# A two-layer decoder trunk on one core: where the partial sums of paired products are kept, and which engine empties the PSUM banks

## The chip, the core and the metric

The kernel runs on one core of one Trainium2 chip. A core has a matrix engine (TensorE, PE in the profile, with its weight loads as PEld), a vector engine (VectorE, DVE), a scalar engine (ScalarE, ACT), a general engine (GpSimd, POOL) and a queue that only issues transfers (SyncE, SP). Matrix products are accumulated in PSUM, which this kernel uses as eight banks of 128 x 512 float32; everything else lives in SBUF. Each engine works through its own instructions in a fixed order and waits for the others at semaphores. The metric is the time of one execution in microseconds (us).

## What is computed

Two layers over 256 positions of width 2048. Each layer normalises the rows, projects them with one wide matrix into queries, keys, values, the two halves of a spatial gating unit and two sets of gates, runs sliding-window attention and the spatial unit, merges both by the gates, and applies an output projection and a SwiGLU feed-forward part of width 5632.

```python
for l in range(DEPTH):
    h = rms_norm(x, mix_norm[l])
    q, k, v, uv, gate_logits = jnp.split(h @ w_in[l], cuts, axis=-1)
    q = apply_rope(rms_norm(q.reshape(B, S, N_Q_HEADS, HEAD_DIM), q_norm[l]), cos, sin)
    k = apply_rope(rms_norm(k.reshape(B, S, N_KV_HEADS, HEAD_DIM), k_norm[l]), cos, sin)
    branch_a = sliding_window_attention(q, k, v, sinks[l]) @ w_attn_branch[l]
    branch_b = chunked_sgu(jax.nn.gelu(uv), w_spatial[l], ...) @ w_sgu_branch[l]
    gates = jax.nn.sigmoid(gate_logits)
    merged = gates[..., :D_MODEL] * branch_a + gates[..., D_MODEL:] * branch_b
    x = x + merged @ w_out[l]
    h2 = rms_norm(x, ffn_norm[l])
    x = x + (jax.nn.silu(h2 @ w_gate[l]) * (h2 @ w_up[l])) @ w_down[l]
```

## The kernel before

**Products in three parts.** The weights are float32. ScalarE rounds a piece of 256 x 512 weights to a high part (`whi`, line 206), VectorE computes the rest (`wlo`, line 207), and the activations are split in the same way (`uh`, `ul`). One product of a 256-row piece with 128 positions is six matmuls: two blocks of 128 rows, each high by high, low by high and high by low (lines 292 to 294). A full *entry* of the work list does this for both halves of the positions (t = 0, 1), so twelve matmuls into two banks.

**The work list.** Every wide matrix is cut into column chunks of 512, and each chunk is a `Plan`: a list of entries, one for each 256 rows. The method `next` of `Stream` runs ahead of the entry in hand: loads by 7 entries, the splits by 4, sums on the weights by 6. Four buffers hold the split weights, so the split of the entry three places ahead starts when TensorE has left the entry before this one.

**Singles and pairs.** The projections of the first part (keys and values, two chunks of queries, gates, `v` and `u` of the spatial unit) and the two branch projections are single plans of X entries. Output projection, gate and up, and down projection are *pairs*: two column chunks `wa` and `wb`, accumulated in banks a[0], a[1] and b[0], b[1] for the two position halves. In a pair, the first 512 rows of the contraction go through the Strassen-Winograd scheme: seven products P1 to P7 of one block in place of eight, with sums of the weights (`k11` to `k22`, line 194) and of the activations (`sh`, `sl`). The other rows are ordinary entries, G into a and U into b. There are 38 pairs in the kernel.

**The head.** P1, P2, P6, P7 and P4 are the head of a pair. They are interleaved with the last four entries t0 to t3 of the plan in front: t0, P1, P2, t1, P6, t2, P7, t3, P4. P5 and P3 come in the body: G, P5, G, P3, then the other G and all U (in pairs marked `by_unit`, G and U come in twos, so that the last G stands third from the end). P1, P6, P7 and P4 accumulate one after the other in a[1], and ScalarE copies the state behind P1, P6 and P7 into SBUF (`snap`, line 318). The final results are a[0] plus the state behind P1; a[1]; b[0] plus the state behind P6 and P5; b[1] plus the state behind P7. P5 goes into b[1], and VectorE adds it to the state of P6 (line 320). Whoever evicts the pair adds the states: `residual` in a second pass over the same rows (line 821), `hidden` by an addition in front of its own work (line 892).

**Banks.** Four banks (`ps_acc`) serve single plans and pairs, taken in turn; two more (`ps_at`) serve attention and, for every other pair, its banks a. The last two hold transpositions.

**Steps by ticks.** Everything that is not a matmul of a plan (rotation of queries, transpositions, softmax, the spatial unit) is registered with `after(n, ...)` and issued n entries later by `tick`. The order of TensorE's instructions is the program's. The order on the other engines is set when the kernel is built, by a planner that estimates when each instruction is ready, so it can differ from the program's.

**Evictions of the first part.** Keys and queries are scaled out of PSUM by VectorE (line 856) into a buffer of the large pool. They are then squared by ScalarE (line 624), scaled by an inverse square root from GpSimd (line 266), rotated, transposed in blocks (line 360), sent through GpSimd's transfers (line 365) and copied into `qT` (line 676), from which the scores are computed (line 692). The masked scores go to SBUF at line 696, and the values are multiplied at line 731. For gelu, VectorE scales half the argument out of PSUM into a temporary (`xh`, line 747), and ScalarE reads PSUM a second time for the square (line 749); both run one or two ticks behind the product. Gates go out of PSUM through a tanh on ScalarE (line 808).

Of the kernel before, what the change touches and what calls it, by code (L numbers as in the profile page):

```python
# [11 lines left out]
ALU = mybir.AluOpType  # L12
# [42 lines left out]
def hybrid_trunk(ctx: ExitStack, tc: tile.TileContext, x, mix_norm, w_in, q_norm, k_norm, sinks,  # L55
# [37 lines left out]
    class Plan:  # L93


        def __init__(self, key, head, body):
            self.key, self.head, self.body = key, head, body
            self.left = len(head) + len(body)
            self.paired = bool(head)
            self.opened, self.acc, self.snaps, self.calls = set(), {}, {}, None  # L100
# [20 lines left out]
    def pair(key, wa, wb, by_unit=False):  # L121

        h1, h2 = 2 * WINO, 2 * WINO + 1
        l11, l12, l21, l22 = (load_of(w, h, t) for w, h, t in ((wa, h1, "k11"), (wb, h1, "k12"), (wa, h2, "k21"),
                                                              (wb, h2, "k22")))
        k11, k12, k21, k22 = l11[0], l12[0], l21[0], l22[0]
        rest = [h for h in range(wa.shape[0] // (2 * P)) if h // 2 != WINO]  # L130
        g, u = [half(wa, h, "G") for h in rest], [half(wb, h, "U") for h in rest]
        head = [dict(tag="P1", loads=[l11, l12], src=k11), dict(tag="P2", loads=[l21, l22], src=k21),
                dict(tag="P6", loads=[], sums=[(k12, k22, "-", k12), (k11, k11, "+", k12)], src=k11),
                dict(tag="P7", loads=[], src=k12), dict(tag="P4", loads=[], sums=[(k21, k21, "-", k11)], src=k21)]
        p5 = dict(tag="P5", loads=[], sums=[(k11, k22, "-", k11)], src=k11)
        p3 = dict(tag="P3", loads=[], src=k22)
        body = [g[0], p5, g[1], p3] + g[2:] + u
        if by_unit:
            body = [g[0], p5, g[1], p3] + u[:2]
            for i in range(2, len(rest), 2):  # L140
                body += g[i:i + 2] + u[i:i + 2]
        return Plan(key, head, body)
# [18 lines left out]
    entries = []  # L161
    for p in plans:
        if p.head:
            t = [entries.pop() for _ in range(4)][::-1]
            h = p.head
            entries += [t[0], h[0], h[1], t[1], h[2], t[2], h[3], t[3], h[4]]
        entries += p.body

    class Stream:
# [19 lines left out]

        def add(self, upto):  # L190
            while self.summed < min(upto, len(entries)):
                for d, x, op, y in entries[self.summed].get("sums", ()):
                    with tc.issue_after(self.last.ins):
                        self.last = nc.vector.tensor_tensor(out=self.raws[d], in0=self.raws[x], in1=self.raws[y],  # L194
                                                            op=ALU.add if op == "+" else ALU.subtract)
                self.summed += 1

        def split(self, upto):
# [97 lines left out]
    def step():  # L296
        e = entries[stream.at]
        p, tag = e["plan"], e["tag"]
        units = units_at[p.key]
        w = stream.next()  # L300
        if tag in "XGU":
            ps = banks(p, "b" if tag == "U" else "a")
            todo = [(ps[t], block(units, e["h"], t)) for t in range(NT)]
        else:
            sh, sl = units[WINO][2:]
            which, t, form = {"P1": ("a", 1, (0, 0)), "P2": ("a", 0, (1, 0)), "P6": ("a", 1, 1), "P7": ("a", 1, 2),
                              "P4": ("a", 1, (1, 1)), "P5": ("b", 1, 0), "P3": ("b", 0, 3)}[tag]
            todo = [(banks(p, which)[t], (sh[:, form], sl[:, form]) if isinstance(form, int)
                     else block(units, 2 * WINO + form[0], form[1]))]
        for ps, u in todo:  # L310
            add_product(p, ps, u, w)
        a, b = p.acc.get("a"), p.acc.get("b")
        if tag in ("P1", "P6", "P7"):
            if tag != "P7":
                p.snaps["s"] = slot([P, 2, CW], name="snap")
            i = {"P1": 0, "P6": 0, "P7": 1}[tag]
            p.snaps[tag] = p.snaps["s"][:, i, :]
            nc.scalar.activation(p.snaps[tag], a[1], AF.Copy)  # L318
        elif tag == "P5":
            nc.vector.tensor_tensor(out=p.snaps["P6"], in0=b[1], in1=p.snaps["P6"], op=ALU.add)  # L320
# [417 lines left out]
    class Spatial:  # L738
# [3 lines left out]
            self.pl, self.nrm = pl, nrm  # L742
            self.vt, self.sguT = [None] * 2, [None] * 2

        def gelu(self, ps, dst, t):
            xh = temp(name="xh")
            nc.vector.tensor_scalar(out=xh, in0=ps[t], scalar1=self.nrm.rh[t], scalar2=None, op0=ALU.mult)
# [5 lines left out]
            nc.vector.scalar_tensor_tensor(out=dst[:, t, :], in0=sq, scalar=1.0, in1=xh,  # L753
                                           op0=ALU.add, op1=ALU.mult)

        def v(self, c, ps):
            self.vt[c] = vt = slot([P, NT, CW], name="v")
            for t in range(NT):
                after(1 + t, lambda t=t: self.gelu(ps, vt, t))
                after(4 + 3 * t, lambda t=t: self.center(c, t))  # L760

        def center(self, c, t):
# [17 lines left out]
            nc.vector.tensor_tensor(out=vt[:, t, :], in0=vt[:, t, :], in1=self.pl.lnb[:, sl], op=ALU.add)  # L780

        def u(self, c, ps):
            ut = slot([P, NT, CW], name="u")
            for t in range(NT):
                after(1 + t, lambda t=t: self.gelu(ps, ut, t))
# [26 lines left out]
    def residual(key, nxt=None, scale=1.0, store=False):  # L812

        def chunk(j, sums):
            for t in range(NT):
                n = 2 if store and j == NCH - 1 else 1
                w = CW // n
                for i in range(n):
                    sl = slice(j * CW + i * w, j * CW + (i + 1) * w)
                    for part in reversed(sums[t]):  # L820
                        nc.vector.scalar_tensor_tensor(out=xs[:, t, sl], in0=part[:, i * w:(i + 1) * w], scalar=scale,  # L821
                                                       in1=xs[:, t, sl], op0=ALU.mult, op1=ALU.add)
# [15 lines left out]
    for l in range(DEPTH):  # L838
# [4 lines left out]
        for kind, c in FIRST_PART:  # L843
# [7 lines left out]
            if kind in ("v", "u"):  # L851
                (spa.v if kind == "v" else spa.u)(c, ps)
            else:
                dst = slot([P, NT, CW], name=kind)
                for t in range(NT):
                    nc.vector.tensor_scalar(out=dst[:, t, :], in0=ps[t], scalar1=norm.r[t], scalar2=None, op0=ALU.mult)
                att.keys(dst) if kind == "kv" else att.queries(c, dst)
            tick()

# [26 lines left out]
        def hidden(hT, c):  # L886
            hid = slot([P, NT, CW], name="hid")

            def added(sums):
                for x in sums:  # L890
                    if len(x) > 1:
                        nc.vector.tensor_tensor(out=x[1], in0=x[0], in1=x[1], op=ALU.add)  # L892
                return [x[-1] for x in sums]

            def on_gate(sums):
                g = added(sums)
# [5 lines left out]
            def on_up(sums):  # L902
                up = added(sums)
# [57 lines left out]
```

## Time and profile before

| | |
|---|---|
| median of 3 runs (least to most) | 2495.94 us (2494.14 to 2498.18) |
| the profiled execution, its own time | 2499.61 us |
| its span, first to last instruction | 2497.9 us |
| granted TensorE clock, mean | 0.995 |
| weight splits, line 206 and line 207 | 1012 each, mean 1058 and 1219 ns |
| sums on the weights, line 194 | 152, mean 1220 ns |
| ScalarE waiting in line 206 for TensorE | 854.7 us |
| moved by DMA | 501.99 MB, mean 201 GB/s |

The profile is one execution, taken on the core. A row of a group gives line, engine, operation, what is written and read, and durations; matmuls overlap, so the distance from one start to the next says more than the length of one. A row of the timeline gives start, length, engine, line, operation and, in brackets, the idle time in front and who ended it. A row "A <- B" of the waits gives the time A stood idle until B, how often and the longest.

### The profile page before, as it was taken

Reading aid. Unit: us, or ns where it says so; the run is one execution under the profiler, and the core shown is the slowest. Engines: PE = TensorE matmul, PEld = TensorE weight load, DVE = VectorE, ACT = ScalarE, POOL = GpSimd, SP = SyncE. Lnnn points to the kernel's source line nnn. Section 1 sums busy time; section 2 is a strip of 40 time slices with the busy share of each in tenths; the row PEclk is TensorE's granted clock in tenths of the full one; section 3 lists DMA queues with packets and bytes.
Section 4 is the critical chain, followed back from the end, with each engine's and each line's share of the span. In section 5 each row is a group of like instructions: output and inputs, shape, how many; then the busy total and the mean of one; then the engine's idle time right before and its main releaser. Section 6 shows DMA issues by size and latency. Waiting matters only on the chain.

```text
span 2497.9 us, 31092 instructions
## 1 busy us (share of the span) xinstructions
PE 2479.3 (99%) x11142; PEld 2050.1 (82%) x11142; DVE 1905.9 (76%) x2281; ACT 1340.8 (54%) x1658; POOL 379.3 (15%) x735
## 2 busy tenths in 40 slices
PE   9999999999999999999999999999999999999999
PEld 7778888888888888888887888888888888888887
DVE  6686556797987788778866865567878777877787
ACT  5455444565655565555644554445655555655564
POOL 2401212131110111011123012221311101110110
PEclk9999999999999999999999999999999999999999
DMA  8745667667665767576776456775767666665764
GB/s 282 219 140 166 192 202 211 203 211 223 191 221 182 223 192 223 180 218 196 228 217 195 137 168 201 207 207 175 238 193 217 204 199 214 200 221 182 223 186 151
DMA packets 271562, 501.99 MB, mean 201 GB/s; under 512 B 25968, under 2 KB 28624, under 8 KB 271408
## 3 DMA queue, kind: packets, MB, share of 16 engines
q1 hardware_dynamic: 248720, 476.90, 62.2%
q0 software_dynamic: 22368, 22.84, 3.1%
q8 instruction: 87, 1.43, 0.2%
q14 instruction: 67, 0.55, 0.1%
q10 hardware_dynamic: 320, 0.27, 0.0%
HBM read 475.27 MB, written 2.10 MB: 191 GB/s over the span
## 4 chain that ended last, share of the span: by engine, by line
PE 97%; DMA 1%; DVE 1%; issue 0%; ACT 0%; POOL 0%; SPq 0%; DVEq 0%; ACTq 0%
PE acc L292 31%; PE acc L293 31%; PE acc L294 31%; PE po L731 1%; DMA tt<-box 1%; PE psc L692 1%; PE pt L402 1%; PE ppt L721 1%; PE psg L795 0%; POOL tt L365 0%; DVE wlo L207 0%; ACT whi L206 0%; DMA raw<-in_w_in_dram 0%; DVE ul L393 0%; PE pw L591 0%
## 5 line engine op out<-in xcount | busy, mean ns | idle before, releaser
L207 DVE TENSOR_TENSOR wlo<-raw,whi 128x1024 fp32r<-128x1024 f32 (+1 forms) x1012 | 1227.7, 1219 | 518.5 <-ACT whi L206 506.4
L206 ACT ACTIVATE whi<-raw 128x1024 fp32r<-128x1024 f32 (+1 forms) x1012 | 1065.5, 1058 | 1029.5 <-PE acc L294 854.7
L292 PE MATMUL acc<-whi,uh 128*128 128x512 f32 x3204 | 1258.6, 393 | 3.1 <-ACT gate L808 1.8
L293 PE MATMUL acc<-wlo,uh 128*128 128x512 f32 x3204 | 1252.6, 391 | 0.8 <-DVE wlo L207 0.8
L294 PE MATMUL acc<-whi,ul 128*128 128x512 f32 x3204 | 1252.0, 391 | 0.0
L292 PEld LDWEIGHTS acc<-whi,uh 128*128 128x128 f32 x3204 | 604.2, 189 | 128.1 <-ACT gate L808 2.2
L293 PEld LDWEIGHTS acc<-wlo,uh 128*128 128x128 f32 x3204 | 604.2, 189 | 127.6 <-DVE wlo L207 3.8
L294 PEld LDWEIGHTS acc<-whi,ul 128*128 128x128 f32 x3204 | 603.9, 188 | 126.2
L365 POOL DMA_DIRECT2D tt<-box x656 | 321.7, 497 | 1724.1 <-DVE box L360 650.0
L194 DVE TENSOR_TENSOR raw<-raw,raw 128x1024 f32<-128x1024 f32 x152 | 185.4, 1220 | 1.0
L292 PE MATMUL acc<-whi,sh 128*128 128x512 f32 x304 | 118.9, 391 | 0.0
L294 PE MATMUL acc<-whi,sl 128*128 128x512 f32 x304 | 118.4, 390 | 0.0
L293 PE MATMUL acc<-wlo,sh 128*128 128x512 f32 x304 | 118.4, 390 | 0.0
L318 ACT ACTIVATE snap<-acc 128x512 f32<-128x512 f32 x114 | 68.2, 598 | 40.6 <-PE acc L294 40.6
L292 PEld LDWEIGHTS acc<-whi,sh 128*128 128x128 f32 x304 | 57.1, 188 | 11.9
L294 PEld LDWEIGHTS acc<-whi,sl 128*128 128x128 f32 x304 | 57.1, 188 | 11.9
L293 PEld LDWEIGHTS acc<-wlo,sh 128*128 128x128 f32 x304 | 57.1, 188 | 11.5
L821 DVE SCALAR_TENSOR_TENSOR xs<-acc,xs 128x512 f32<-128x512 f32 (+1 forms) x66 | 42.5, 667 | 9.2 <-PE acc L294 8.9
L892 DVE TENSOR_TENSOR snap<-acc,snap 128x512 f32<-128x512 f32 x66 | 45.2, 685 | 4.8 <-PE acc L294 4.8
L821 DVE SCALAR_TENSOR_TENSOR xs<-snap,xs 128x512 f32<-128x512 f32 (+1 forms) x50 | 33.0, 662 | 1.4 <-ACT snap L318 1.3
L905 DVE SCALAR_TENSOR_TENSOR hid<-snap,rr,hid 128x512 f32<-128x512 f32 x44 | 32.5, 739 | 0.0
L709 ACT ACTIVATE pr<-pr,negm 128x128 f32<-128x128 f32 (+1 forms) x64 | 28.2, 442 | 7.9 <-DVE negm L702 7.9
(134 smaller groups left out, 884.7 us busy)
## 6 DMA issues: line engine op xcount, KB each, us to landing
raw<-in_w_in_dram SPq DMA_DIRECT2D x239, 512.0 KB, 4.2
raw<-in_w_up_dram SPq DMA_DIRECT2D x176, 512.0 KB, 5.0
raw<-in_w_gate_dram SPq DMA_DIRECT2D x176, 512.0 KB, 4.4
raw<-in_w_down_dram SPq DMA_DIRECT2D x176, 512.0 KB, 4.5
raw<-in_w_out_dram SPq DMA_DIRECT2D x64, 512.0 KB, 4.7
tt<-box POOLq DMA_DIRECT2D x656, 32.0 KB, 4.3
raw<-in_w_attn_branch_dram SPq DMA_DIRECT2D x32, 512.0 KB, 4.0
raw<-in_w_sgu_branch_dram SPq DMA_DIRECT2D x32, 512.0 KB, 4.5
```

What stands on the lines that cost most here:

```text
L194: self.last = nc.vector.tensor_tensor(out=self.raws[d], in0=self.raws[x], in1=self.raws[y], op=ALU.add if op == "+" else ALU.subtract)
L206: nc.scalar.activation(hi[:, i, :], raw[:, i, :], AF.Copy)
L207: self.last = nc.vector.tensor_tensor(out=lo[:, i, :], in0=raw[:, i, :], in1=hi[:, i, :].bitcast(F32), op=ALU.subtract)
L292: nc.tensor.matmul(ps, a, hi[:, kk, :], start=first and kk == 0, stop=False, skip_group_check=True)
L293: nc.tensor.matmul(ps, a, lo[:, kk, :], start=False, stop=False, skip_group_check=True)
L294: nc.tensor.matmul(ps, b, hi[:, kk, :], start=False, stop=kk == 1, skip_group_check=True)
L318: nc.scalar.activation(p.snaps[tag], a[1], AF.Copy)
L365: nc.gpsimd.dma_start(dst[j * B:(j + 1) * B, i], box[i * B:(i + 1) * B, j])
L709: nc.scalar.activation(pr4[:, h, :nk], pr4[:, h, :nk], AF.Exp, bias=nm_[:, h:h + 1], accum_out=den[:, h:h + 1])
L821: nc.vector.scalar_tensor_tensor(out=xs[:, t, sl], in0=part[:, i * w:(i + 1) * w], scalar=scale, in1=xs[:, t, sl], op0=ALU.mult, op1=ALU.add)
L892: nc.vector.tensor_tensor(out=x[1], in0=x[0], in1=x[1], op=ALU.add)
L905: nc.vector.scalar_tensor_tensor(out=hid[:, t, :], in0=up[t], scalar=norm.rr[t], in1=hid[:, t, :], op0=ALU.mult, op1=ALU.mult)
```

## The change

Which products are computed does not change; where their sums are kept does.

- P5 joins the head and goes into the empty bank a[0]. Five entries of the plan in front are interleaved: t0, P1, t1, P5, t2, P2, P6, t3, P7, t4, P4.
- Behind P5, ScalarE copies P5 from a[0] to SBUF (`kept`) and then a[1] (the state behind P1) into a[0]. P2 accumulates onto that.
- Behind P6 and P7, VectorE reads a[1], adds P5 and writes the two halves of `kept`.
- Behind the second G entry (the first, in pairs by units) ScalarE copies the halves of `kept` into b[0] and b[1], and P3 and the U entries accumulate onto them. All additions at the eviction go.
- The sums on the weights are four differences instead of three and one sum, since the products come in another order.
- Keys, queries and the halves of gelu's argument leave PSUM through ScalarE, the latter at the end of the product; the square is taken from the half in SBUF, and the gelu result overwrites it.

```diff
+        head = [dict(tag="P1", loads=[l11, l12], src=k11),
+                dict(tag="P5", loads=[], sums=[(k11, k12, k11)], src=k11),
+                dict(tag="P2", loads=[l21, l22], src=k21),
+                dict(tag="P6", loads=[], sums=[(k11, k22, k11)], src=k11),
+                dict(tag="P7", loads=[], sums=[(k12, k22, k12)], src=k12),
+                dict(tag="P4", loads=[], sums=[(k21, k21, k11)], src=k21)]
-        body = [g[0], p5, g[1], p3] + g[2:] + u
+        body = g[:2] + [g[2], p3] + g[3:] + u
+        g[1]["then"] = "open"
         if by_unit:
-            body = [g[0], p5, g[1], p3] + u[:2]
+            body = g[:2] + [p3] + u[:2]
+            g[0]["then"] = g[1].pop("then")
...
-            t = [entries.pop() for _ in range(4)][::-1]
+            t = [entries.pop() for _ in range(5)][::-1]
             h = p.head
-            entries += [t[0], h[0], h[1], t[1], h[2], t[2], h[3], t[3], h[4]]
+            entries += [t[0], h[0], t[1], h[1], t[2], h[2], h[3], t[3], h[4], t[4], h[5]]
...
-        if tag in ("P1", "P6", "P7"):
-            if tag != "P7":
-                p.snaps["s"] = slot([P, 2, CW], name="snap")
-            i = {"P1": 0, "P6": 0, "P7": 1}[tag]
-            p.snaps[tag] = p.snaps["s"][:, i, :]
-            nc.scalar.activation(p.snaps[tag], a[1], AF.Copy)
-        elif tag == "P5":
-            nc.vector.tensor_tensor(out=p.snaps["P6"], in0=b[1], in1=p.snaps["P6"], op=ALU.add)
+        if tag == "P5":
+            p.kept = slot([P, 2, CW], name="kept")
+            nc.scalar.activation(p.kept[:, 1, :], a[0], AF.Copy)
+            nc.scalar.activation(a[0], a[1], AF.Copy)
+        elif tag in ("P6", "P7"):
+            nc.vector.tensor_tensor(out=p.kept[:, int(tag == "P7"), :], in0=a[1], in1=p.kept[:, 1, :], op=ALU.add)
+        if "then" in e:
+            for t, ps in enumerate(banks(p, "b")):
+                nc.scalar.activation(ps, p.kept[:, t, :], AF.Copy)
+                p.opened.add(id(ps))
         p.left -= 1
         if e is getattr(p, "last_g", None):
-            p.calls[0]([[a[0], p.snaps["P1"]], [a[1]]])
+            p.calls[0](a)
         if p.left == 0 and p.paired:
-            p.calls[1]([[b[0], p.snaps["P6"]], [b[1], p.snaps["P7"]]])
+            p.calls[1](b)
...
+        def half(self, ps, name):
+            dst = slot([P, NT, CW], name=name)
+            for t in range(NT):
+                nc.scalar.activation(dst[:, t, :], ps[t], AF.Copy, scale=self.nrm.rh[t])
+            return dst
...
-            nc.scalar.activation(sq, ps[t], AF.Square, scale=self.nrm.r[t])
+            nc.scalar.activation(sq, xh, AF.Square, scale=2.0)
...
-                    nc.vector.tensor_scalar(out=dst[:, t, :], in0=ps[t], scalar1=norm.r[t], scalar2=None, op0=ALU.mult)
+                    nc.scalar.activation(dst[:, t, :], ps[t], AF.Copy, scale=norm.r[t])
```

In `residual` the second pass over `snap` goes, and in `hidden` the function `added` with its additions.

More of the change, by code (lines that the diff above doesn't have):

```diff
@@ L99, in __init__ @@
             self.paired = bool(head)
-            self.opened, self.acc, self.snaps, self.calls = set(), {}, {}, None
+            self.opened, self.acc, self.calls = set(), {}, None
             for e in head + body:
@@ L131, in pair @@
         g, u = [half(wa, h, "G") for h in rest], [half(wb, h, "U") for h in rest]
[L132 to L135, printed above, removed]
+        head = [dict(tag="P1", loads=[l11, l12], src=k11),
[4 more added lines that the diff above has]
+                dict(tag="P4", loads=[], sums=[(k21, k21, k11)], src=k21)]
         p3 = dict(tag="P3", loads=[], src=k22)
-        body = [g[0], p5, g[1], p3] + g[2:] + u
+        body = g[:2] + [g[2], p3] + g[3:] + u
+        g[1]["then"] = "open"
         if by_unit:
-            body = [g[0], p5, g[1], p3] + u[:2]
+            body = g[:2] + [p3] + u[:2]
+            g[0]["then"] = g[1].pop("then")
             for i in range(2, len(rest), 2):
@@ L191, in add @@
             while self.summed < min(upto, len(entries)):
-                for d, x, op, y in entries[self.summed].get("sums", ()):
+                for d, x, y in entries[self.summed].get("sums", ()):
                     with tc.issue_after(self.last.ins):
                         self.last = nc.vector.tensor_tensor(out=self.raws[d], in0=self.raws[x], in1=self.raws[y],
-                                                            op=ALU.add if op == "+" else ALU.subtract)
+                                                            op=ALU.subtract)
                 self.summed += 1
@@ L306, in step @@
             which, t, form = {"P1": ("a", 1, (0, 0)), "P2": ("a", 0, (1, 0)), "P6": ("a", 1, 1), "P7": ("a", 1, 2),
-                              "P4": ("a", 1, (1, 1)), "P5": ("b", 1, 0), "P3": ("b", 0, 3)}[tag]
+                              "P4": ("a", 1, (1, 1)), "P5": ("a", 0, 0), "P3": ("b", 0, 3)}[tag]
             todo = [(banks(p, which)[t], (sh[:, form], sl[:, form]) if isinstance(form, int)
@@ L743, in __init__, with gelu @@
             self.vt, self.sguT = [None] * 2, [None] * 2
-        def gelu(self, ps, dst, t):
-            xh = temp(name="xh")
-            nc.vector.tensor_scalar(out=xh, in0=ps[t], scalar1=self.nrm.rh[t], scalar2=None, op0=ALU.mult)
+        def half(self, ps, name):
[3 more added lines that the diff above has]
+            return dst
+        def gelu(self, dst, t):
+            xh = dst[:, t, :]
             sq = temp(name="sq")
-            nc.scalar.activation(sq, ps[t], AF.Square, scale=self.nrm.r[t])
+            nc.scalar.activation(sq, xh, AF.Square, scale=2.0)
             nc.vector.scalar_tensor_tensor(out=sq, in0=sq, scalar=1.0 / GELU_A, in1=xh,
@@ L752, in gelu @@
             nc.scalar.activation(sq, sq, AF.Tanh, scale=2.0 * GELU_C * GELU_A)
-            nc.vector.scalar_tensor_tensor(out=dst[:, t, :], in0=sq, scalar=1.0, in1=xh,
-                                           op0=ALU.add, op1=ALU.mult)
+            nc.vector.scalar_tensor_tensor(out=xh, in0=sq, scalar=1.0, in1=xh, op0=ALU.add, op1=ALU.mult)
         def v(self, c, ps):
-            self.vt[c] = vt = slot([P, NT, CW], name="v")
+            self.vt[c] = vt = self.half(ps, "v")
             for t in range(NT):
-                after(1 + t, lambda t=t: self.gelu(ps, vt, t))
+                after(1 + t, lambda t=t: self.gelu(vt, t))
                 after(4 + 3 * t, lambda t=t: self.center(c, t))
@@ L782, in u @@
         def u(self, c, ps):
-            ut = slot([P, NT, CW], name="u")
+            ut = self.half(ps, "u")
             for t in range(NT):
-                after(1 + t, lambda t=t: self.gelu(ps, ut, t))
+                after(1 + t, lambda t=t: self.gelu(ut, t))
             for b in range(2):
@@ L819, in chunk @@
                     sl = slice(j * CW + i * w, j * CW + (i + 1) * w)
-                    for part in reversed(sums[t]):
-                        nc.vector.scalar_tensor_tensor(out=xs[:, t, sl], in0=part[:, i * w:(i + 1) * w], scalar=scale,
-                                                       in1=xs[:, t, sl], op0=ALU.mult, op1=ALU.add)
+                    nc.vector.scalar_tensor_tensor(out=xs[:, t, sl], in0=sums[t][:, i * w:(i + 1) * w], scalar=scale,
+                                                   in1=xs[:, t, sl], op0=ALU.mult, op1=ALU.add)
                     if store:
@@ L887, in hidden, with on_gate @@
             hid = slot([P, NT, CW], name="hid")
[L889 to L896, printed above, removed]
+            def on_gate(g):
                 for t in range(NT):
@@ L900, in on_gate, with on_up @@
                     nc.vector.scalar_tensor_tensor(out=th, in0=th, scalar=1.0, in1=g[t], op0=ALU.add, op1=ALU.mult)
-            def on_up(sums):
-                up = added(sums)
+            def on_up(up):
                 for t in range(NT):
```

## The prediction

> **What bounds the kernel now.** I read the page's first line of engines, then the busy time by stretches, then TensorE's own waits.
>
> ```profile
> span 2497.9 us, 31092 instructions
> ...
> PE 2479.3 (99%) x11142; PEld 2050.1 (82%) x11142; DVE 1905.9 (76%) x2281; ACT 1340.8 (54%) x1658; POOL 379.3 (15%) x735
> ```
>
> TensorE (PE) is busy in 2479.3 of 2497.9 us. VectorE (DVE) and ScalarE (ACT), which the change relieves and loads, have a quarter and a half of the span free. The next rows give busy time by stretches; the columns are the stretch, its length, busy us of PE, PEld, DVE, ACT, POOL with instructions in brackets, then the granted clock, DMA share and GB/s.
>
> ```profile
> 99.00:107.00 8.00, 6.25 (x24) 4.74 (x24) 6.42 (x9) 2.18 (x3) 1.40 (x1) 0.79 0.60 184
> 127.00:138.00 11.00, 8.17 (x30) 6.62 (x29) 5.45 (x13) 5.19 (x15) 0.00 (x0) 0.69 0.39 116
> 1339.00:1346.00 7.00, 5.33 (x20) 4.00 (x19) 5.50 (x9) 2.09 (x3) 0.26 (x1) 0.76 0.61 181
> 1366.00:1377.00 11.00, 8.17 (x30) 6.60 (x29) 5.77 (x12) 4.73 (x14) 0.00 (x0) 0.69 0.43 131
> 1698.00:1709.00 11.00, 9.23 (x40) 7.27 (x40) 9.29 (x10) 7.26 (x11) 0.00 (x0) 1.00 0.35 99
> 460.00:1255.00 795.00, 795.00 (x3536) 658.70 (x3535) 658.45 (x729) 457.52 (x532) 95.27 (x194) 1.00 0.66 207
> ```
>
> The last row is a whole layer's paired products, where nearly all the edits lie: TensorE is busy in all 795 us, at full clock. There is nothing to win there, because the change keeps every matmul. TensorE's waits, in us in total, times, longest:
>
> ```profile
> PE po L731 <- DVE pr L696: 5.7, 2, 2.8
> PE psc L692 <- ACT qT L676: 3.4, 2, 1.7
> PE acc L292 <- ACT gate L808: 1.8, 1, 1.8
> ```
>
> That is 10.9 us. The waits of lines 692 and 731 lie in the first four stretches, and the clock falls behind them: (1 - 0.79) x 8 = 1.7 us, 0.31 x 11 = 3.4, 0.24 x 7 = 1.7 and again 3.4 us, 10.2 together. So 21 us, 0.8%, is the most that this change could win, and only if it removes all these waits.
>
> **The change, part by part.** First the instructions. Columns: count, durations in ns (least/median/most), first and last start, forms.
>
> ```profile
> L318 ACT ACTIVATE snap<-acc x114: 575/598/602, 462.3 to 2465.5; 128x512 f32<-128x512 f32 x114
> L892 DVE TENSOR_TENSOR snap<-acc,snap x66: 679/684/692, 594.8 to 2437.1; 128x512 f32<-128x512 f32 x66
> ...
> L821 DVE SCALAR_TENSOR_TENSOR xs<-snap,xs x50: 417/684/694, 463.0 to 2476.6; 128x512 f32<-128x512 f32 x46, 128x256 f32<-128x256 f32 x4
> ...
> L320 DVE TENSOR_TENSOR snap<-acc,snap x38: 648/683/690, 480.1 to 2474.5; 128x512 f32<-128x512 f32 x38
> ```
>
> There are 38 pairs. VectorE loses 66 + 50 + 38 = 154 additions and gets 2 x 38 = 76: some 78 x 0.68 = 53 us less. ScalarE loses 114 copies and gets 4 x 38 = 152: 38 x 0.6 = 23 us more. Three of the four new copies write PSUM. No row shows ScalarE doing that; nearest are this copy out of PSUM, 0.60, and a scaled one (line 808 below), 0.68; I take 0.6, and the ends move nothing, as the next parts show. The four sums on the weights per pair stay four. Saved and added time is worth nothing by itself, since TensorE covers both engines; what counts is the few places where TensorE now waits for a copy or an addition.
>
> Time unit of a head: each product is six matmuls. In the pair at 884 us, P1 begins at the first row, and four products (P1, P2, and the two of a whole entry) later P6 begins:
>
> ```profile
> 884.43 0.39 PE L292 MATMUL acc<-whi,uh 128*128 128x512 f32 x1
> ...
> 889.87 0.39 PE L292 MATMUL acc<-whi,sh 128*128 128x512 f32 x1
> ```
>
> So four products take 5.44 us, one 1.36, a whole entry 2.72.
>
> *P5, two copies, then P2.* The copies run one after the other, and entry t2 (2.72 us) lies between P5 and P2. ScalarE's rows around the P1 copy of before:
>
> ```profile
> 884.67 1.06 ACT L206 ACTIVATE whi<-raw 128x1024 fp32r<-128x1024 f32 x1 [1.66 <-PE acc L294]
> 885.99 0.60 ACT L318 ACTIVATE snap<-acc 128x512 f32<-128x512 f32 x1 [0.25 <-PE acc L294]
> ```
>
> ScalarE stands idle until P1 ends (884.43 + 1.36 = 885.79) and starts 0.2 us later. So 0.2 + 2 x 0.6 = 1.4 us, or 2.5 with one weight split (1.06) in front: both below 2.72. Cost 0. Without the cover it would be 1.4 x 38 = 53 us. What is queued behind the waiting copies is the next split, whose result is due three entries later.
>
> *P6, addition, then P7.* Here VectorE, not ScalarE, releases the bank. Its rows:
>
> ```profile
> 885.77 1.23 DVE L207 TENSOR_TENSOR wlo<-raw,whi 128x1024 fp32r<-128x1024 f32 x1 [0.69 <-ACT whi L206]
> 887.56 2.36 DVE L207 TENSOR_TENSOR wlo<-raw,whi 128x1024 fp32r<-128x1024 f32 x2 [0.57 <-ACT whi L206]
> 889.84 1.22 DVE L194 TENSOR_TENSOR raw<-raw,raw 128x1024 f32<-128x1024 f32 x1
> ```
>
> Back to back these go every 1.14 us (887.56 to 889.84 is two). From the start of P2: the high part starts at 0.24 (884.67 - 884.43), the low part 1.10 after it (885.77 - 884.67) at 1.34, then the sum for P4 at 2.48, the low part of the entry three after P6 at 3.62, the addition at 4.76. It ends at 5.44. P7 is due P2 + P6 + t3 = 5.44 us after the same start. **The margin is nil**: 0 to 0.1 us for each head; I take 0, as the chain adds no more than rounding.
>
> Eight heads have more in that stretch. Behind a pair ordered by units, the previous pair's last G entry is t2 itself, so its eviction (two 128x512 operations of VectorE, or two tanh and two of them) falls there. VectorE has 0.69 us idle in front of the low part at 885.77, which takes the first; the second (0.6 at its pitch, like the 0.68 of line 821) starts 0.1 before 1.34 and pushes the chain by 0.5. So 8 x 0.5 = 4.0 us, bounds 0 (the planner puts the addition first) and 8 x 1.2 = 9.6 (neither hidden).
>
> *P7, addition, then P4*: behind P7 only one low part is queued, so 0.2 + 1.14 + 0.68 fits in 2.72 with 0.7 to spare. *The two copies that open b*: they need the previous pair's two evictions, now two operations instead of four, and have an entry and more before P3. Cost 0. The loads are the same and in the same order; SP's queue keeps its buffers. P2's two loads come later against it, yet DMA is at 0.66 in the row above.
>
> *Evictions moved to ScalarE.* Twelve of keys and queries and 16 of gelu's argument:
>
> ```profile
> L808 ACT ACTIVATE gate<-acc,rhalf x32: 667/686/692, 111.0 to 1701.0; 128x512 f32<-128x512 f32 x32
> L856 DVE TENSOR_SCALAR q<-acc,rstd x8: 733/738/745, 58.6 to 1328.7; 128x512 f32<-128x512 f32 x8
> ```
>
> Equal within 0.05 us each. The question is whether the chain behind the two attention waits gets shorter. Second queries, layer 1:
>
> ```profile
> 1325.72 1.29 DVE L360 STREAM_TRANSPOSE box<-q 128x512 f32<-128x512 f32 x2
> ...
> 1328.05 1.39 DVE L856 TENSOR_SCALAR q<-acc,rstd 128x512 f32<-128x512 f32 x2
> 1336.33 2.93 POOL L266 TENSOR_TENSOR rq<-ssq,neg_half 128x16 f32<-128x16 f32 x1
> 1368.02 1.13 ACT L676 ACTIVATE qT<-tt 128x512 f32<-128x512 f32 x2
> 1369.29 0.75 DVE L696 TENSOR_TENSOR pr<-psc,mask 128x256 f32<-128x256 f32 x2
> ```
>
> The eviction runs behind the transposition of the first queries, and GpSimd's square root only at 1336.33, behind the first queries' transfers. A microsecond gained at 1328 dies there. I take 0, with one weight split's slot (2.7 us) a layer to either side, since the planner may put line 676 one split earlier or later.
>
> *Gate wait, layer 1.* The head now begins behind the gate's last entry, not one entry later:
>
> ```profile
> 1700.41 1.25 ACT L808 ACTIVATE gate<-acc,rhalf 128x512 f32<-128x512 f32 x2
> 1701.13 0.51 PE L292 MATMUL acc<-whi,uh 128*128 128x512 f32 x1 [1.77 <-ACT gate L808]
> ```
>
> P1 waited for that eviction; now the entry behind P1 needs the bank, 1.36 us earlier than P1 did. If ScalarE keeps its place the wait is 3.1; if the planner evicts at once, it is gone. -1.8 to +1.4; I take 0.
>
> **Sum**: 4.0 + 0. The profiled execution took 2499.61 us (span 2497.9), 3.7 above the median of the runs, 2495.94. On its own base it gives 2503.6; on the median 2499.9: **2500.0**.
>
> **Rivals.**
>
> 1. *Slower.* The addition after P6 is queued behind one more operation in every head. Rows of before for the addition after P5, which had no deadline:
>
> ```profile
> 904.55 1.22 DVE L434 TENSOR_TENSOR ul<-flat,uh 128x1024 fp32r<-128x1024 f32 x1
> 905.68 0.70 DVE L360 STREAM_TRANSPOSE box<-hid 128x512 f32<-128x512 f32 x1
> 906.31 0.65 DVE L320 TENSOR_TENSOR snap<-acc,snap 128x512 f32<-128x512 f32 x1
> ```
>
> It came after two such operations. For it: the nil margin. Against: in the heads few such operations are due. It decides as soon as one 0.65 us operation stands in front: 38 x 0.65 = 25 us, 2521; half the heads, 2508.
>
> A price on that: the rows above lose 1.7 to 3.4 us of clock behind waits of 1.7 to 2.8 us, yet none behind 1.8 us at 1701 (clock 1.00). If the clock fell behind each of the eight waits of my sum, they would cost 8 x (0.5 + 1.7) = 18 us, 2514. The Trainium skill ("TensorE: Matmul & The Clock Gate", What's actually happening) has the clock halved only after about an idle window of 3.4 us; by it 0.5 us costs 0.5. The trace agrees at 1701 but not at 127, where a 2.8 us wait was followed by 0.69.
>
> 2. *Faster.* The second queries come one split earlier in both layers: the waits on line 731 (5.7) go with their clock loss (3.4 each), 5.7 + 2 x 3.4 = 12.5, so 4.0 - 12.5 on the median: 2487.4. For it: ScalarE has the argument ready for its own square (line 624). Against: GpSimd's queue above.
>
> 3. *Later attention.* The same chain a split later: 2 x 2.7 more, 2505.
>
> 4. *No change at all.* The planner puts the addition in front in the eight heads too, so the paired products stay as they are (PE 795.00 of 795.00): 2496. Against: the eviction was issued before it.
>
> **Chances.** Own sum 0.35 (2496 to 2504); rival 4 0.15 (2493 to 2499); rival 1 0.25, from 2503 up; rival 2 0.13; rival 3 0.12. Within 0.2% (5 us, about what a measurement of this kernel can tell from no change), that is 2491 to 2501: two thirds of the sum's, all of rival 4 and a little of the others, 0.45. Slower 0.41, faster 0.14. Range 2487 to 2514: it takes in the bounds of the eight heads, the gate and the attention chain and the point of rival 2, and leaves out the upper half of rival 1 and what lies beyond rival 2.
>
> **What will show it.** TensorE's waits should list line 292 behind the new VectorE addition, some eight times about 0.5 us, and no copy of ScalarE. VectorE's busy time should fall by about 74 us (53, and 28 evictions at 0.74), ScalarE's rise by about 42 (23, and 28 at 0.68). The addition after P6 should end 5.4 us after P2's start. I am wrong if TensorE waits in all 38 heads, if it waits for the copies, or if lines 692 and 731 no longer wait.

## The result: 0.5% slower, 2510.2 us, and the profile after

| | before | after |
|---|---|---|
| median (least to most) | 2497.01 us, 4 runs | 2510.20 us (2505.35 to 2512.88), 4 runs |
| the profiled execution, its own time | 2499.61 us | 2510.53 us |
| ratio, 95% interval | | 1.0052 [1.0034, 1.0071] |

A second measurement of the same two kernels on another chip gave 2509.90 against 2496.16 us, a ratio of 1.0055 [1.0042, 1.0069]. The prediction was 2500.0, range 2487 to 2514. The time lies in the range; the point is 10 us low, and "within 0.2%", to which it gave the highest chance, did not happen.

In the listing of the kernel after, lines stand a little lower: the matmuls are 296 to 298, the splits 210 and 211, the sums on the weights 198, the copies behind P5 are 319 (into `kept`) and 320 (a[1] into a[0]), the additions 322, the copies that open b 325, and the evictions of `residual` 832. The page of the kernel after begins:

```profile
span 2508.8 us, 31194 instructions
...
PE 2484.9 (99%) x11142; PEld 2045.2 (82%) x11142; DVE 1842.5 (73%) x2175; ACT 1381.8 (55%) x1724; POOL 384.9 (15%) x735
...
L322 DVE TENSOR_TENSOR kept<-acc,kept 128x512 f32<-128x512 f32 x76 | 52.0, 684 | 0.3 <-PE acc L298 0.3
...
L325 ACT ACTIVATE acc<-kept 128x512 f32<-128x512 f32 x76 | 43.7, 586 | 5.3 <-DVE kept L322 5.3
```

VectorE is 63 us less busy, ScalarE 41 us more, and the kernel is slower: neither engine's total set the time. (The prediction said 74 and 42. It added recorded durations; VectorE's operations overlap by 0.08 us when they run back to back, 1.22 us long at a distance of 1.14, and busy time counts the overlap once. The recorded durations alone fell by 71.6 us.) The stretch of paired products that was full before (795.00 of 795.00) now has a hole of 2.6 us, at full clock:

```profile
460.00:1255.00 795.00, 792.41 (x3509) 652.00 (x3508) 631.21 (x687) 465.38 (x547) 95.59 (x194) 1.00 0.65 206
```

TensorE's waits, in us in total, times, longest:

```profile
PE po L737 <- DVE pr L702: 5.7, 2, 2.8
PE psc L698 <- ACT qT L682: 3.3, 2, 1.7
PE acc L296 <- DVE kept L322: 2.5, 5, 0.5
...
PE acc L296 <- ACT gate L820: 1.5, 1, 1.5
PE acc L296 <- ACT acc L320: 1.4, 4, 0.4
```

The attention waits are the same as before. New are the addition (line 322) and the copy (line 320), 3.9 us together. That is too little for a loss of 11 us in the span. The view counts idle time from the recorded end of the matmul before, and that end lies 0.16 us after the next matmul is due (a length of 0.39 us at a distance of 0.23): shorter waits are missing, and longer ones stand there 0.16 us too short. TensorE's own rows show the rest. This is the timeline of the pair whose P6 starts at 892.09: VectorE first, then TensorE at the start of P7 (the first `sh` row).

```profile
892.02 1.23 DVE L211 TENSOR_TENSOR wlo<-raw,whi 128x1024 fp32r<-128x1024 f32 x1 [0.53 <-ACT whi L210]
893.16 1.22 DVE L198 TENSOR_TENSOR raw<-raw,raw 128x1024 f32<-128x1024 f32 x1
894.30 1.22 DVE L211 TENSOR_TENSOR wlo<-raw,whi 128x1024 fp32r<-128x1024 f32 x1
895.43 0.69 DVE L322 TENSOR_TENSOR kept<-acc,kept 128x512 f32<-128x512 f32 x1
```

```profile
890.73 0.39 PE L296 MATMUL acc<-whi,uh 128*128 128x512 f32 x1
...
895.94 0.39 PE L298 MATMUL acc<-whi,ul 128*128 128x512 f32 x1
896.27 0.47 PE L296 MATMUL acc<-whi,sh 128*128 128x512 f32 x1
896.57 0.40 PE L297 MATMUL acc<-wlo,sh 128*128 128x512 f32 x1
```

Undisturbed matmuls start every 0.227 us. P2 starts at 890.73, so P7 is due 5.44 later, at 896.17. The addition ends at 895.43 + 0.69 = 896.12, before that; but P7 starts at 896.27, 0.15 us after the addition's end. So the step to P7 is 0.33 in place of 0.23, and the next one 0.30: 0.10 us of wait and some 0.08 lost behind it. No view of waits lists this, and it happens in 25 heads.

To find all such places I summed, over the trace, the distance from each product matmul's start to the next start beyond 0.227 us. "Pairs" are the stretches of the paired products of both layers, "first part" what lies before them in each layer:

| us beyond the pitch | first part, layer 0 | first part, layer 1 | pairs |
|---|---|---|---|
| before | 17.3 | 12.0 | 3.5 |
| after | 16.0 | 12.3 | 14.7 |

All of the loss lies in the pairs, 11.2 us. Of the 14.7, P7 waits in 30 of 38 heads: 25 times 0.10 to 0.15 (2.7 us together) and five times 0.67 (3.3 us), each followed by the 0.08 (2.4). In four heads P2 waits 0.51 for the copy of line 320 and then loses 0.11 (2.5). The gate wait has 1.7, against 2.0 before.

The four copies, ScalarE's rows and TensorE's P2 (in brackets the idle time in front):

```profile
1794.00 0.60 ACT L319 ACTIVATE kept<-acc 128x512 f32<-128x512 f32 x1 [2.97 <-PE acc L298]
1794.49 2.00 ACT L210 ACTIVATE whi<-raw 128x1024 fp32r<-128x1024 f32 x2
1796.39 0.59 ACT L320 ACTIVATE acc<-acc 128x512 f32<-128x512 f32 x1
```

```profile
1797.04 0.50 PE L296 MATMUL acc<-whi,uh 128*128 128x512 f32 x1 [0.35 <-ACT acc L320]
```

Two splits (x2, 2.00 us) stand between the two copies, so the second ends at 1796.98. In the pair at 888 only one split stands there, and nothing waits. Those four heads have no wait at P7, since they have already lost more than its 0.10.

One of the five heads with 0.67, on VectorE: the previous pair's last evictions (line 832) stand in the chain, as the prediction had it, and no idle time is left from there to the addition.

```profile
761.48 1.22 DVE L198 TENSOR_TENSOR raw<-raw,raw 128x1024 f32<-128x1024 f32 x1
762.61 0.68 DVE L832 SCALAR_TENSOR_TENSOR xs<-acc,xs 128x512 f32<-128x512 f32 x1
763.21 1.22 DVE L211 TENSOR_TENSOR wlo<-raw,whi 128x1024 fp32r<-128x1024 f32 x1
764.34 0.68 DVE L832 SCALAR_TENSOR_TENSOR xs<-acc,xs 128x512 f32<-128x512 f32 x1
764.95 1.22 DVE L211 TENSOR_TENSOR wlo<-raw,whi 128x1024 fp32r<-128x1024 f32 x1
...
768.35 0.68 DVE L322 TENSOR_TENSOR kept<-acc,kept 128x512 f32<-128x512 f32 x1
```

### The profile page after: what moved, and what is told of

Its sections match the earlier page's. It is cut to its first block, busy times and chain, and to the rows that moved or that the text cites. A ratio compares the mean times of both kernels' runs of the same rounds, so it can differ in the third digit from the quotient of the medians.

```text
span 2508.8 us, 31194 instructions
## 1 busy us (share of the span) xinstructions
PE 2484.9 (99%) x11142; PEld 2045.2 (82%) x11142; DVE 1842.5 (73%) x2175; ACT 1381.8 (55%) x1724; POOL 384.9 (15%) x735
## 5 line engine op out<-in xcount | busy, mean ns | idle before, releaser
L322 DVE TENSOR_TENSOR kept<-acc,kept 128x512 f32<-128x512 f32 x76 | 52.0, 684 | 0.3 <-PE acc L298 0.3
L325 ACT ACTIVATE acc<-kept 128x512 f32<-128x512 f32 x76 | 43.7, 586 | 5.3 <-DVE kept L322 5.3
L903 ACT ACTIVATE hid<-acc,rhalf 128x512 f32<-128x512 f32 x44 | 30.4, 690 | 19.2 <-PE acc L298 19.1
L737 PEld LDWEIGHTS po<-kv,pT 128*128 128x128 f32 x192 | 25.3, 203 | 7.5 <-ACT qT L682 6.4
```

The lines of the kernel that those rows point to most:

```text
L322: nc.vector.tensor_tensor(out=p.kept[:, int(tag == "P7"), :], in0=a[1], in1=p.kept[:, 1, :], op=ALU.add)
L325: nc.scalar.activation(ps, p.kept[:, t, :], AF.Copy)
```

## The experiments

The theory after this reading: the whole loss is the head's order. TensorE reaches P7 as soon as the addition behind P6 is done or sooner, and each operation added in front of that addition shows in full. Rivals: the evictions moved to ScalarE cost the time, or the 0.10 us are rounding of the records and hide some slack.

**1. The pairs changed alone.** The kernel after, with keys, queries and gelu's argument evicted as before.

```diff
-                    nc.scalar.activation(dst[:, t, :], ps[t], AF.Copy, scale=norm.r[t])
+                    nc.vector.tensor_scalar(out=dst[:, t, :], in0=ps[t], scalar1=norm.r[t], scalar2=None, op0=ALU.mult)
...
-            self.vt[c] = vt = self.half(ps, "v")
+            self.vt[c] = vt = slot([P, NT, CW], name="v")
```

> The new banks and order of the pairs alone; keys, queries and gelu's argument leave PSUM as before. Theory (the loss is TensorE's short waits in the heads of the pairs: for the addition behind P6 in some 30 of 38 heads, for the copy into a[0] in a few): all of the 13 us stay, 2507 to 2512 us where before takes 2497, and TensorE waits some 11 us more than before between pairs. Rival (ScalarE's new evictions delay other work in the first part of a layer): 2497 to 2500 us.

Measured: 2509.30 us, 1.0050 [1.0037, 1.0063]. The pairs lose 14.7 us, as in the kernel after.

**2. The evictions changed alone.** The kernel before, with ScalarE's evictions.

```diff
-                    nc.vector.tensor_scalar(out=dst[:, t, :], in0=ps[t], scalar1=norm.r[t], scalar2=None, op0=ALU.mult)
+                    nc.scalar.activation(dst[:, t, :], ps[t], AF.Copy, scale=norm.r[t])
...
-            nc.scalar.activation(sq, ps[t], AF.Square, scale=self.nrm.r[t])
+            nc.scalar.activation(sq, xh, AF.Square, scale=2.0)
```

> The kernel before with the ScalarE evictions of keys, queries and half of gelu's argument alone. Theory (heads): no change, 2495 to 2499 us, and the two attention waits stay at about 5.7 and 3.4 us. Rival (evictions cost): 2503 to 2510 us, with the attention waits or their clock losses longer.

Measured: 2498.67 us, 1.0010 [1.0001, 1.0018]; the pairs lose 3.5 us as before, and the attention waits keep their 5.7 and 3.3 us. So the loss belongs to the pairs. The evictions alone cost 0.1%, by the interval at most 0.2%.

**3. P6 in front of P2.** If the chain to the addition is a little too long, one product more between P6 and P7 removes every wait on it.

```diff
-                dict(tag="P2", loads=[l21, l22], src=k21),
-                dict(tag="P6", loads=[], sums=[(k11, k22, k11)], src=k11),
+                dict(tag="P6", loads=[l21, l22], sums=[(k11, k22, k11)], src=k11),
+                dict(tag="P2", loads=[], src=k21),
```

> The changed kernel with P6 ahead of P2 in the head, so that P2 and t3 (4.08 us instead of 2.72) lie between P6 and P7, and P6 and t2 between P5 and P2. Theory: the addition behind P6 and the copy into a[0] are both done in time, the waits of the heads go (all of 8.5 and 2.5 us), 2496 to 2500 us. Rival 1 (the copies into PSUM or the smaller slack of the weight splits cost by themselves): 2505 us or more. Rival 2 (the wait moves on to P4 or P3): TensorE's list names line 322 in front of another product, 2502 to 2508.

Measured: 2492.74 us, 0.9987 [0.9978, 0.9996], less than both kernels and 3 us below the range expected. TensorE's waits:

```profile
PE psc L698 <- ACT qT L682: 3.3, 2, 1.7
PE po L737 <- DVE pr L702: 2.8, 1, 2.8
...
PE acc L296 <- ACT acc L320: 1.1, 3, 0.4
```

No wait for line 322 is left, and the pairs lose 4.2 us, almost the 3.5 of before. Three waits for the copy stay, now in front of P6. The gain over before is elsewhere: one of the two waits of line 737, layer 1's, is gone. Line 737 needs one of the two attention banks, and these hold scores until VectorE's additions of line 702 have read them. TensorE finished these scores 11 us before the additions; what makes the additions late is their place in VectorE's order. The kernel after:

```profile
1361.89 0.72 PE L698 MATMUL psc<-kT,qT 64*128 64x128 f32 x8
```

```profile
1369.81 1.23 DVE L211 TENSOR_TENSOR wlo<-raw,whi 128x1024 fp32r<-128x1024 f32 x1 [1.49 <-ACT whi L210]
1372.52 1.22 DVE L211 TENSOR_TENSOR wlo<-raw,whi 128x1024 fp32r<-128x1024 f32 x1 [1.49 <-ACT whi L210]
1373.66 0.75 DVE L702 TENSOR_TENSOR pr<-psc,mask 128x256 f32<-128x256 f32 x2
```

With P6 in front they stand one low part earlier, behind the one that is at 1369.81 in the kernel after:

```profile
1366.89 1.23 DVE L211 TENSOR_TENSOR wlo<-raw,whi 128x1024 fp32r<-128x1024 f32 x1 [1.49 <-ACT whi L210]
1368.03 0.75 DVE L702 TENSOR_TENSOR pr<-psc,mask 128x256 f32<-128x256 f32 x2
```

The first part of layer 1 loses 5.7 us beyond the pitch instead of 12.3: the wait of 2.8 and the clock behind it.

**4. One operation taken out of the chain.** The sum of weights for P4, which VectorE does in front of the addition behind P6, is asked for one entry earlier.

```diff
             h = p.head
+            t[4]["sums"] = h[5].pop("sums")
             entries += [t[0], h[0], t[1], h[1], t[2], h[2], h[3], t[3], h[4], t[4], h[5]]
```

> The changed kernel with the weight sum for P4 issued one entry earlier, in P2's predecessor: one VectorE operation of 1.14 us less in the queue in front of the addition behind P6, all else equal. Theory (the queue in front of the addition decides): the waits for line 322 go in nearly all heads (about 8.5 us), those for the copy into a[0] (2.5) stay, 2500 to 2503 us. Rival (TensorE pays for the dependency itself, whenever the addition ends): 2508 to 2512 us, with 0.1 us still in front of P7 in every head.

Measured: 2498.07 us, 1.0008 [0.9999, 1.0017]. The rows of the same pair on VectorE (lines are one higher here):

```profile
891.30 1.22 DVE L199 TENSOR_TENSOR raw<-raw,raw 128x1024 f32<-128x1024 f32 x1
892.43 2.36 DVE L212 TENSOR_TENSOR wlo<-raw,whi 128x1024 fp32r<-128x1024 f32 x2
894.70 0.68 DVE L323 TENSOR_TENSOR kept<-acc,kept 128x512 f32<-128x512 f32 x1
```

The sum now fills what was idle time in front of a low part, the addition comes earlier, and the 25 short waits are gone. The pairs lose 11.3 us instead of 14.7, less of a gain than the 8.5 us of all waits at P7. The short waits had cost 4.7 us. Six heads keep 0.08 of it each, 0.5 us together: there the addition ends 0.14 us before P7 is due, P7 does not wait, and the second matmul still comes late. Another 0.9 us came back in places too small to name. The five waits of 0.67 stay, because VectorE has no idle time in those heads, so that the order of what stands in front changes nothing; the four for the copy stay too. The rest of the gain, which took the total below the range expected, is again layer 1's wait of line 737, which this edit doesn't touch by its meaning. The additions (line 703 here) again stand one low part earlier, and the copy of the second queries (line 683) only comes behind them:

```profile
1367.99 0.75 DVE L703 TENSOR_TENSOR pr<-psc,mask 128x256 f32<-128x256 f32 x2
```

```profile
1369.44 1.14 ACT L683 ACTIVATE qT<-tt 128x512 f32<-128x512 f32 x2
```

So that copy, from which the prediction and the expectations of experiment 9 reckon this wait, is not on its path.

**5. The cover of the copies taken away.** P2 directly behind P5.

```diff
-            entries += [t[0], h[0], t[1], h[1], t[2], h[2], h[3], t[3], h[4], t[4], h[5]]
+            entries += [t[0], h[0], t[1], h[1], h[2], t[2], h[3], t[3], h[4], t[4], h[5]]
```

> The kernel after, with P2 directly behind P5 (order t0, P1, t1, P5, P2, t2, P6, t3, P7, t4, P4): the cover of the two copies of ScalarE is taken away, and P7 comes one entry later behind P6 than ... no, as late as before. Theory (the copies cost nothing only because entry t2 lies beside them): P2 waits for the copy of line 320 in every head, 0.2 + 2 x 0.6 = 1.4 us where the two copies are adjacent, 2.3 where one weight split stands between them as in the kernel after: 38 x 1.4 = 53 to 38 x 2.3 = 87 us more, so about 2550 to 2585. If the clock falls behind waits of this length, more. Rival (the copies are cheap, an unseen path covers them): at most 2515.

Measured: 2612.73 us, 1.0465 [1.0450, 1.0480]; 28 us above the upper end of what I expected. The wait, and four stretches by windows (the last three numbers are clock, DMA share and GB/s):

```profile
PE acc L296 <- ACT acc L320: 85.8, 38, 3.5
```

```profile
599.76:603.17 3.41, 1.29 (x6) 0.77 (x5) 3.20 (x3) 2.21 (x4) 0.00 (x0) 1.00 0.48 154
603.17:606.59 3.42, 3.42 (x10) 2.65 (x9) 1.31 (x2) 1.06 (x1) 0.00 (x0) 0.50 0.55 146
644.13:647.55 3.42, 2.23 (x10) 1.50 (x8) 2.84 (x4) 2.33 (x4) 0.00 (x0) 1.00 0.21 31
647.55:650.96 3.41, 2.48 (x11) 2.06 (x12) 2.13 (x2) 1.67 (x3) 0.00 (x0) 1.00 0.38 129
```

In 33 heads the wait is 2.28 us by the distance of starts, which is one split between the copies, the upper price that I had named (38 x 2.3 = 87). Five heads wait 3.2 to 3.6. On top comes 0.11 us behind each wait and the clock: behind eight of the 33 equal waits, and four of the five longer ones, TensorE ran at half rate for 3.41 us, as from 603.17 on; that cost 1.5 to 1.7 us each time, about 20 us in all. So the copies do cost 2.3 us a head where nothing covers them; the entry t2 hides that in 34 of 38 heads.

**6. Two operations more in front of the addition.** Two unused 128x256 operations on VectorE behind P6.

```diff
+            if tag == "P6":
+                with tc.issue_after(stream.last.ins):
+                    for _ in range(2):
+                        nc.vector.tensor_tensor(out=idle, in0=idle, in1=idle, op=ALU.max)
```

> The kernel after, with two unused 128x256 operations of VectorE (about 0.34 us each) queued in front of the addition behind P6 in every head. Theory (nothing is left between the end of that addition and the start of P7): nearly all of 0.68 shows in each of 38 heads, 20 to 26 us, so 2530 to 2536; the waits of line 296 for line 322 rise to some 0.7 to 0.8 each. Rival (0.1 us waits are a rounding of the records and there is slack): under 5 us, at most 2515.

Measured: 2520.98 us, 1.0098 [1.0084, 1.0113], about half of the cost expected. VectorE's rows say why:

```profile
895.82 1.22 DVE L211 TENSOR_TENSOR wlo<-raw,whi 128x1024 fp32r<-128x1024 f32 x1
896.95 0.42 DVE L327 TENSOR_TENSOR idle<-idle 128x256 f32<-128x256 f32 x1
897.29 0.68 DVE L328 TENSOR_TENSOR kept<-acc,kept 128x512 f32<-128x512 f32 x1
...
899.02 0.42 DVE L327 TENSOR_TENSOR idle<-idle 128x256 f32<-128x256 f32 x1
```

The planner left one of the two in front (0.34 by its pitch, 897.29 - 896.95) and put the other behind. P7's waits grew from 0.10 to 0.44 and from 0.67 to 1.0, by 0.34 in each of the 30 heads, 10.1 us of the 12.0 by which the pairs grew (14.7 to 26.7). Slack would have swallowed some of the 0.34. There is none.

**7. and 8. Attention's due times.** The first chunk's scores two entries later, in the kernel of experiment 3 and in the kernel before.

```diff
-            n = Q_FIRST + (4 * Q_STEP - 8) * c
+            n = Q_FIRST + 2 + (4 * Q_STEP - 10) * c
```

> The kernel with P6 in front of P2 (2492.7), and the first chunk's scores two entries later in each layer. Theory (the attention waits of TensorE are a matter of the due times of these steps, and the lower granted clock behind them comes from them): the waits of lines 698 and 737 go, 6 us, and some 3 to 7 us of clock with them: 2480 to 2487. Rival (the wait only moves on to the next of the chain, or the clock is low there for another reason): 2490 to 2495.

> The kernel before, with the first chunk's scores two entries later in each layer, nothing else. Theory (the attention waits and the clock behind them are 9.1 + 10.2 us and have nothing to do with this change): 2478 to 2488. Rival (the chain behind the queries is late whatever the due time, or the low clock stays): 2493 to 2497.

Measured: 2498.02 us, 1.0007 [0.9999, 1.0016], and 2499.69 us, 1.0012 [1.0003, 1.0021]. Both theories fell, and both times lie a few us above what the rivals allowed as well, which was not followed up. The waits moved on with the steps, here in the kernel before with later scores:

```profile
PE psc L692 <- ACT qT L676: 3.3, 2, 1.7
PE po L731 <- DVE pr L696: 3.2, 2, 2.8
PE po L731 <- DVE den L711: 3.0, 2, 1.5
```

Scores came 5 us later, and so did line 676: at 1345.74 in place of 1340.35, again directly behind a split, with the same 1.7 us of wait. A later due time for the consumer doesn't help here, because the planner places the copy later too. What decides its place was not settled.

**9. P6 in front, evictions as before.** Experiments 1 and 3 together.

> P6 in front of P2, and the evictions of keys, queries and gelu's argument left with VectorE as in the kernel before. Theory (the time comes from the order of the head alone, and the evictions are worth nothing): the paired products lose some 4 us beyond the pitch of 227 ns, as with P6 first and ScalarE's evictions, and the total is 2490 to 2497, decided by where the second queries of layer 1 land (their wait of 2.8 us and its clock, 6.5 us together, or not). Rival (ScalarE's evictions bring what the reordered kernel gained): 2498 or more.

Measured: 2493.56 us, 0.9989 [0.9980, 0.9998], the same as experiment 3 within the intervals. Layer 1's wait of line 737 is gone here as well, with the additions of line 702 one low part earlier, so ScalarE's evictions are not what removed it.

**10. The residual's evictions later.** In the kernel after, the first evictions of a pair of the down projection are asked for two entries later, to clear the five heads of 0.67.

```diff
-            product_pair(key, lambda sums: chunk(j, sums), lambda sums: chunk(j + 1, sums))
+            late = nxt is None and not store or key[0] == "hid" and j + 2 < NCH
+            first = (lambda sums: after(2, lambda j=j, sums=list(sums): chunk(j, sums))) if late else (lambda sums: chunk(j, sums))
+            product_pair(key, first, lambda sums: chunk(j + 1, sums))
```

> The kernel after, with the first chunk's eviction of the down projection's pairs issued two entries later, behind the addition of P6. Theory (the five longest waits of line 296, 0.67 us each, come from the two operations of line 832 that stand in front of the chain to that addition): these five fall to about 0.1 us, 2.9 us in all and nothing else of the pairs changes: 2505 to 2509. Rival (the five come from something else, or VectorE takes the time elsewhere): five waits of about 0.67 us stay, 2509 to 2512.

Measured: 2506.98 us, 1.0043 [1.0031, 1.0056]. The time is the one expected, by luck: the reason is wrong. VectorE's rows of the head shown above, and P7:

```profile
767.97 1.28 DVE L832 SCALAR_TENSOR_TENSOR xs<-acc,xs 128x512 f32<-128x512 f32 x2
769.16 1.22 DVE L211 TENSOR_TENSOR wlo<-raw,whi 128x1024 fp32r<-128x1024 f32 x1
770.30 0.68 DVE L322 TENSOR_TENSOR kept<-acc,kept 128x512 f32<-128x512 f32 x1
```

```profile
771.13 0.47 PE L296 MATMUL acc<-whi,sh 128*128 128x512 f32 x1 [1.13 <-ACT whi L210]
```

The planner moved both evictions only until just in front of the addition, where no idle time swallows any of them: 0.10 + 2 x 0.6 = 1.3 us, in six heads. (The bracket names a split; the addition that ends at 770.98, 0.15 before P7, is what P7 waited for.) The pairs lose 19.1 us, 4.4 more than after. The total is lower because layer 1's wait of line 737 went once more (first part of layer 1: 5.7 in place of 12.3). That the two operations of line 832 make the five waits is thus borne out by their price, not by their going.

**11. The kernel after again** on the chip of 9 and 10, as their measure.

> The kernel after once more, unchanged, on the chip of the two runs beside it, as their measure: 2505 to 2513, a ratio to before of 1.0034 to 1.0071.

Measured: 2509.90 us, 1.0055; pairs 14.6 us, with the same 30 and four waits.

## Why the prediction was ten microseconds low

**Right.** The kernel is bound by TensorE and could win nothing in the pairs. Of the eight heads with evictions in t2, five wait, all behind a pair of the down projection: 5 x (0.67 + 0.08) = 3.7 us against the 4.0 of the sum. Behind the two by-unit pairs of gate and up, and in one more head, there is no wait. A PSUM copy of ScalarE takes 0.59 us against the 0.6 taken. The copies that open b make TensorE wait nowhere. The attention waits stayed, and the gate wait fell by 0.3. The evictions gave nothing.

Two of these terms came out by luck. For the eight heads I had 8 x 0.5; five waited, and for longer, since the wait in every head stands on top. And the attention term was read from the wrong chain: the additions of line 696 at 1369.29 in the kernel before read scores that TensorE had finished at 1358.2, so the second queries, their eviction and GpSimd's queue do not set that wait. VectorE's order does, and it happened to stay as it was.

**The step that failed: "The margin is nil: 0 to 0.1 us for each head; I take 0".** The chain was right to a few hundredths (the addition ends 5.39 us after P2's start, 5.44 was worked out), but the step went from the addition's end to P7's start without the release. I had charged 0.2 us from TensorE's end to ScalarE's start for the copies, from a row of before, and nothing the other way. It is 0.15, and each wait loses another 0.08 at the next matmul. So a nil margin costs 0.18 a head, outside the bound of 0.1; in 25 heads 2.7 + 2.0 = 4.7 us. The heads of the kernel after and of experiments 4 and 6 bear this out over a wide span (the margin is the time from the addition's end to P7's due start; both by starts):

| margin, us | wait of P7 | lost behind it |
|---|---|---|
| -0.86 (experiment 6) | 1.00 | 0.08 |
| -0.52 | 0.67 | 0.08 |
| -0.29 (experiment 6) | 0.43 | 0.08 |
| 0.00 | 0.15 | 0.08 |
| 0.05 | 0.10 | 0.08 |
| 0.14 (experiment 4) | 0.00 | 0.08 |
| 0.24 | 0.00 | 0.01 |

**A second one: "Cost 0" for the copies behind P5.** One split in front was counted (2.5 of the 2.72 us of t2). In four heads the planner put two between the copies: 4 x 0.62 = 2.5 us, and "no copy of ScalarE" among the waits was wrong. With 0.22 us to spare, this was not a step to put at nothing in all 38 heads.

Together: 3.7 + 4.7 + 2.5 = 10.9 of the 11.2 us of the pairs, where the sum had 4.0. The medians differ by 13.2. The prediction's base was also 1.1 us low: its median of before, 2495.94, became 2497.01 with a fourth run. The profiled execution of before lay 3.7 us above its median of then, which the prediction took off, and that of after only 0.3 above; the 2 us that are left were not located (the mean granted clock of the two profiled executions, 0.995 and 0.996, points that way).

**The rivals.** Rival 1 came nearest: a wait in nearly all heads, 34 of 38. Of the signs of being wrong that the prediction named, waits for the copies came (in four heads), and a wait in all 38 nearly did. Its mechanism, one more operation in front, wasn't the one; experiments 6 and 10 show that its price per operation was right. Its clock price (18 us) did not appear in the kernel after: the windows give 1.00 over the pairs, with waits at P7 of 0.67 at most. By the Trainium skill ("TensorE: Matmul & The Clock Gate", What's actually happening) the clock drops only after an idle window of about 3.4 us, and for 0.5 us that came true. Rival 2, 6 us for one layer, did not come with this change but did with experiments 3, 4, 9 and 10, none of which touches attention by its meaning. Its mechanism, the second queries coming earlier, isn't the one: in experiment 4 their copy stands behind the additions, and the wait is gone all the same. Why the planner moves the additions was not settled.

## What to carry to other kernels

Where one engine must release another just in time, count both directions of the release and the loss behind the wait: a margin of almost zero is a cost per pass (0.18 us here), and by the table above it takes about 0.25 us of margin to call it nothing. Such waits are shorter than the view of waits lists; distances between starts show them. And where a planner orders the other engines' queues, an edit moves more than it names: look at which wait moved before believing the total, as experiments 4 and 10 show.

## What the runs showed beside the question

- A wait of 2.28 us is enough for the clock to fall, but not always: it fell behind 8 of 33 such waits in one execution. The trace's clock record shows which. In experiment 5's paired products every fall lasts 3.41 us, and the falls start whole multiples of 3.41 us apart. Summed by starts on this grid, TensorE had stood idle for 1.99 us or more in each of the 12 stretches that were followed by half rate, and for 1.90 or less in all others. The wait that ends at 602.27 lay in one stretch (599.76 to 603.17, half rate behind it); the one that ends at 648.48 was divided between two and cost no clock. So a wait's place on the grid decides as well as its length. The idle window of about 3.4 us that the Trainium skill ("TensorE: Matmul & The Clock Gate", What's actually happening) gives, taken as idle throughout, would leave all of them at full clock; its remarks that the window runs freely and is 3413 ns long agree with the record.
- Executions of one kernel differ along with their mean granted clock: the kernel before took 2492.2 us at 0.999 and 2498.4 to 2501.9 at 0.995, the kernel after 2505.4 at 0.998 and 2512.9 at 0.995. A difference of 3 us needs many executions.
- Behind a wait, the second matmul comes late too: 0.08 us behind the waits for VectorE, 0.11 behind those for ScalarE's copy.
